# Out-projection weights and first token pairs, prepared in half-tile steps inside the last merge

## The chip, the cores and the metric

The kernel runs on one core of one Trainium2 chip. The metric is the device time of one execution in microseconds (us); lower is better. Every time below comes from the kernel before: three timed runs, and one further execution taken with the hardware profiler, whose trace is the source of all durations.

The engines have these names in the profile: PE does matmuls (PEld is its weight load), DVE is the vector engine, ACT the scalar engine, POOL the general one, SP the engine whose queue issues most transfers. L161 is line 161 of the kernel. Each engine works through its own queue in a fixed order. That order is written at compile time: the framework's scheduler walks the program in the order in which it was traced, with a cost model of its own, and places an instruction when the model says that its inputs are there. What the model takes to be ready sooner than it is on the chip makes the engine wait, with everything behind it.

## The reference, cut to what matters

One inference layer over 2,048 sample tokens and 128 prompt tokens of width 1,024. Three mixers (a gated delta rule, a spatial gating unit, a Fourier mixer) run from one input projection. Their outputs are projected back to the model width, gated and added; this sum goes through one output projection, is scaled per channel, added to the input rows and normalised:

```python
pb = jnp.einsum('btnw,nwd->btnd', br, w_branch)
gt = jax.nn.sigmoid(gates.reshape(B, T, N_BRANCH, D_MODEL))
merged = jnp.einsum('btnd,btnd->btd', gt, pb)
out = jnp.einsum('btd,de->bte', merged, w_out)
...
h = h + gate * out            # gate: one row of 1024 values per request group
y = rmsnorm(h, final_g)
```

## The kernel before, in words

All large products are done in pairs of float16 numbers: a float32 operand is scaled by a power of two and split into a high part (ACT copies it to float16) and a low part (DVE subtracts the high part); a product is then three matmuls (high·high, high·low, low·high). The power of two comes from a sum of squares: ACT squares the block with an accumulator, DVE casts the 128 sums to bfloat16, PE adds them over the partitions with a matrix of ones (the *scale product*, in `scales`, L178), and DVE makes the scale from the exponent bits.

**The merges (L1362).** Three passes, one per mixer branch (1, 2, then 0), each over 8 blocks of 128 channels (`db`) and, in each block, five token tiles (512, 512 and 128 tokens of the second half and 512, 512 of the first; the last pass takes the second half first). One tile is a gate product (24 matmuls against `xh`, `xl`), a sigmoid on ACT (L1389), a branch product (12 matmuls against `o16`), a scaling on DVE (L1398) and an addition on POOL (L1399). The merged rows go to DRAM (`mD`, printed as `mrg`). Weights of the following blocks are read into the two buffers `wst` and converted along the way.

**Work between the tiles of the last merge.** After each of its 40 tiles the last merge takes one step of a generator (`next(work, 0)`, L1401). First come the rest of `gate_rows` (the per-channel output gate from `w_ada`). Then `out_weights` (L1516) prepares W_out in 8 column blocks `i`:
- `block(i)` (L1457) loads the block (`ost`, 512 KB) and its gate row;
- `squared` (L1464) squares it on ACT, takes its scale product and its scale;
- `ungated` (L1473) splits the block and stores both halves in DRAM (`uD`, printed as `uw`; the prompt tile uses these), multiplies the block by the gate row and squares it again.

When all eight are done, one more sum and scale product (`osc`, L1528) give the scale of the gated W_out, and `quarters` (L1491) forms seven weight matrices from the four quarters of W_out: a product of a 2×2 block matrix in seven block products instead of eight. Four of them stay in SBUF (`gq`), three go to DRAM (`twD`, printed as `tw`). The float16 results of `squared`, `ungated` and `stored` all come from one tag `t16` with two buffers.

`kept` (`tc.keep_in_program_order`) pins an instruction behind what was traced before it on its engine. In the kernel before, ACT and DVE work on W_out is pinned; the scale products on PE are not.

**The out-projection (L1623).** Sixteen sample tiles are taken in eight pairs. For each pair `m_load` reads the merged rows, `m_scale` makes the pair's scale, POOL forms four sums (`pair_sums`, L1559), `pair_operands` (L1570) splits seven operands into `xl`, and seven products of 12 matmuls each (`formed`) are joined on DVE into the input rows `ha`, `hb` (L1658), which then get their norm. Pair 0 is loaded and summed near the end of the last merge, as soon as its half is stored (`ahead_out`, L1588). Pair 1, the input rows, the `tw` matrices and the final norm's row are loaded after the merge; pair 1 and the rows into a pool `op` that opens only then. The prompt tile (16) is an ordinary product with the blocks from `uD`, at the end.

Of the kernel before, what the change touches and what calls it, by code (L numbers as in the profile page):

```python
# [10 lines left out]
F32 = mybir.dt.float32  # L11
# [100 lines left out]
def hybrid_flow_kernel(ctx: ExitStack, tc: tile.TileContext, x_prompt, x_sample, state_delta, c, c_ctx, ln_g, w_ada,  # L112
# [47 lines left out]
    def mm(out, l, r, start=True, stop=True):  # L160
        PE.matmul(out, l, r, start=start, stop=stop)  # L161
# [16 lines left out]
    def scales(ss, pl, tag, sb16=None):  # L178
# [4 lines left out]
        V.tensor_copy(t[:, 0:1], ps)  # L183
# [1178 lines left out]
    def merge(n, first, inv, each=None, halves=HALVES, mid=None, then=None, work=iter(())):  # L1362

        steps, sinv = iter(()), None
        for db in range(KT):
# [8 lines left out]
            for h0, hn, tbs in halves:  # L1374
# [5 lines left out]
                for t0, tn in tbs:  # L1380
# [7 lines left out]
                    with tc.high_priority():  # L1388
                        A.activation(sg, ps, AF.Sigmoid, scale=gw.inv)  # L1389
                    ps = bank(ps_mm, [P, tn])  # L1390
# [66 lines left out]
    def block(i):  # L1457
        st = sb(orp, [P, KT, P], "ost", bufs=3)
        SY.dma_start(st, w_out[0][:, i * P:(i + 1) * P].rearrange("(k p) c -> p k c", p=P))
        gr = sb(orp, [P, P], "ogr", bufs=3)  # L1460
        SY.dma_start(gr, gateD[0:1, i * P:(i + 1) * P].to_broadcast([P, P]))
        return i, st, gr.rearrange("p (o c) -> p o c", o=1).to_broadcast([P, KT, P])

    def squared(i, st, gr):  # L1464
        ss = sb(orp, [P, 1], "uss", bufs=2)
        kept(A.activation(half16(), st, AF.Square, accum_out=ss))
        us_, inv = scales(ss, orp, "usc2")
        V.tensor_copy(uinv[:, i:i + 1], inv)
        us1 = sb(orp, [P, 1], "us1", bufs=2)
        V.tensor_copy(us1, us_)  # L1470
        return i, st, gr, us1

    def ungated(i, st, gr, us_):  # L1473
        hi, lo = half16(), half16()
        kept(A.activation(hi, st, AF.Copy, scale=us_))
        kept(V.scalar_tensor_tensor(lo, st, us_, hi, ALU.mult, ALU.subtract))
        for l, t in enumerate((hi, lo)):
            SY.dma_start(uD[i][:, l], t.rearrange("p k c -> p (k c)"))
        kept(V.tensor_tensor(st, st, gr, ALU.mult))
        kept(A.activation(half16(), st, AF.Square, accum_out=wos[:, i:i + 1]))  # L1480

    def paired(hi, lo, src):
        kept(A.copy(hi, src))
        kept(V.tensor_tensor(lo, src, hi, ALU.subtract))

    def stored(n, j, src):
        t = sb(orp, [P, 2, 4, P], "t16", F16, bufs=2)
        paired(t[:, 0], t[:, 1], src)
        SY.dma_start(twD[:, n, j], t.rearrange("p l k c -> p (l k c)"))

    def quarters(i, st, gr):  # L1491
        j = i % 4
        kept(V.scalar_tensor_tensor(st, st, wsc[0], gr, ALU.mult, ALU.mult))
        if i < 4:
            paired(gq[:, 0:2, j, 0], gq[:, 0:2, j, 1], st.rearrange("p (n k) c -> p n k c", n=2))
            yield
            return
        x_, y_ = st[:, 0:4], st[:, 4:8]
        sub = lambda out, a, b: kept(V.tensor_tensor(out, a, b, ALU.subtract))
        paired(gq[:, 2, j, 0], gq[:, 2, j, 1], y_)  # L1500
        t = sb(ep, [P, 4, P], "st", bufs=3)
        sub(t, y_, x_)
        stored(1, j, t)
        yield
        sub(x_, x_, gq[:, 0, j, 0])
        sub(x_, x_, gq[:, 0, j, 1])
        stored(0, j, x_)
        sub(y_, y_, x_)
        yield
        paired(gq[:, 3, j, 0], gq[:, 3, j, 1], y_)  # L1510
        sub(x_, gq[:, 1, j, 0], y_)
        kept(V.tensor_tensor(x_, x_, gq[:, 1, j, 1], ALU.add))
        stored(2, j, x_)
        yield

    def out_weights():  # L1516
        for _ in gates:
            yield
        read, sq = None, None
        for i in range(KT + 2):  # L1520
            was, sq = sq, squared(*read) if read is not None else None
            read = block(i) if i < KT else None
            if was is not None:
                ungated(*was)
            yield
        order_ = [0, 4, 1, 5, 2, 6, 3, 7]
        nxt = block(order_[0])
        V.tensor_reduce(wos[:, KT:KT + 1], wos[:, 0:KT], AX.X, ALU.add)  # L1528
        wsc.extend(scales(wos[:, KT:KT + 1], orp, "osc"))
        yield  # L1530
        for i in order_[1:] + [None]:
            now, nxt = nxt, block(i) if i is not None else None
            yield from quarters(*now)
# [4 lines left out]
    def m_load(t, pl, tag):  # L1538
        mt = sb(pl, [P, KT, P], tag, bufs=4 if tag == "mt" else 2)
        SY.dma_start(mt, mD[:, :, t * P:(t + 1) * P].rearrange("k p t -> p k t"))  # L1540
        return mt

    def m_scale(mts, by=None):
        jk = half16()
        ss = sb(orp, [P, 3], "mss", bufs=2)
        for i, mt in enumerate(mts):
            A.activation(jk, mt, AF.Square, accum_out=ss[:, i:i + 1])
        if len(mts) > 1:
            V.tensor_add(ss[:, 2:3], ss[:, 0:1], ss[:, 1:2])
        s, inv = scales(ss[:, 2:3] if len(mts) > 1 else ss[:, 0:1], orp, "msc")  # L1550
        minv = sb(orp, [P, 1], "minv", bufs=3)
        V.tensor_copy(minv, inv) if by is None else V.tensor_mul(minv, inv, by)
        return s, minv
# [5 lines left out]
    def pair_sums(a, b):  # L1559
        s, minv = m_scale([a, b], wsc[1])  # L1560
        yield
        sf = [sb(orp, [P, 2, 4, P], "ost", bufs=3) for _ in range(2)]
        a11, a12, a21, a22 = a[:, 0:4], a[:, 4:8], b[:, 0:4], b[:, 4:8]
# [6 lines left out]
    def pair_operands(i, a, b, sf, s, minv):  # L1570
        v = xl.rearrange("p k t -> p (k t)")[:, (i % 2) * 7168:(i % 2 + 1) * 7168].rearrange("p (l s k c) -> p l s k c", l=2, s=7, k=4)
        operands.append((v, minv))
        halved(v[:, 0, 0:2].rearrange("p s k c -> p (s k) c"), v[:, 1, 0:2].rearrange("p s k c -> p (s k) c"), a, s)
        yield
# [3 lines left out]
        halved(v[:, 0, 2], v[:, 1, 2], b[:, 4:8], s)  # L1578
# [18 lines left out]
    tw = xh.rearrange("p k t -> p (k t)")[:, 0:12288].rearrange("p (n j l k c) -> p n j l k c", n=3, j=4, l=2, k=4)  # L1597
    for n in range(3):
        SY.dma_start(tw[:, n].rearrange("p j l k c -> p j (l k c)"), twD[:, n])
    op = pool(ctx, "op", 2)  # L1600
    loaded = [m_load(t, op, "mt") for t in PAIRS[1]]

    def rows_of(t):
        hh = sb(op, [P, D], "hh", bufs=5)
        SY.dma_start(hh, xrows(t * P, P))
        return hh
# [16 lines left out]
    for i_, (ta, tb) in enumerate(PAIRS):  # L1623
# [5 lines left out]
        def coming():  # L1629
            if i_ == 0:  # L1630
                yield from pair_sums(*loaded)
            nx = [m_load(t, op, "mt") for t in PAIRS[i_ + 2]] if i_ + 2 < len(PAIRS) else None
# [49 lines left out]
        if i_ == len(PAIRS) - 3:  # L1682
            mt = m_load(16, op, "mt")
            s, minv = m_scale([mt])
            mh, ml = half16(), half16()
            halved(mh, ml, mt, s)
# [7 lines left out]
        if i_ >= len(PAIRS) - 2:  # L1694
            for i in range(4):
# [49 lines left out]
```

## Time and profile before

| | us |
|---|---|
| timed runs: median of 3 | 2208.57 |
| lowest, highest | 2205.6, 2211.82 |
| the profiled execution's own time | 2209.94 |
| its span (first to last instruction) | 2208.2 |
| PE busy in the span | 2110.2 |
| DVE, ACT, POOL busy | 1404.9, 1054.3, 728.7 |

The span ends with the last output transfer; the 1.7 us between the span and the execution's own time lie around it. The last merge runs from about 1735 to 2024 us, the out-projection from there to the end. A wait is put down to the engine and line that ended it. "PEclk" is the clock that the power control granted to PE, 1.00 being full speed.

### The profile page before, as it was taken

The page shows a single profiled execution, that of the slowest core. Times are in us where ns is not written, and L with a number is a line of the kernel's source. Part 1 is how long each engine was busy: PE and PEld are TensorE (multiplying, and loading weights), DVE is VectorE, ACT ScalarE, POOL GpSimd, SP SyncE. Part 2 cuts the span into 40 slices and gives each one's busy share as a digit, 9 for nine tenths or more (in the row PEclk, how much of TensorE's full clock was granted, in tenths as well). Part 3 has the DMA queues.
Part 4 walks back from the last instruction along what each step waited for, and adds up shares of the span by engine and source line. Part 5 has one row for each costly group of instructions (what it writes and reads, how often), then busy time and mean ns, then how long its engine had stood idle before and what let it go on. Part 6 is the DMA issues. An engine that isn't in the chain of part 4 may idle for free.

```text
span 2208.2 us, 43079 instructions
## 1 busy us (share of the span) xinstructions
PE 2110.2 (96%) x16275; PEld 1212.1 (55%) x16275; DVE 1404.9 (64%) x3229; ACT 1054.3 (48%) x2419; POOL 728.7 (33%) x870
## 2 busy tenths in 40 slices
PE   7999999999999998999899999999999999799898
PEld 3564444455555587877455565556554444344344
DVE  5736745479879698666655556756664534763874
ACT  3545644445565474554544445655543324322541
POOL 1421433223334325332322323345432212123742
PEclk9999999999999999999999999999999999999999
DMA  8424733277787664534655556766755535546552
GB/s 280 145 81 163 256 105 109 70 211 230 230 252 224 189 186 149 145 124 130 204 175 148 168 172 184 244 197 199 212 165 169 169 109 191 170 151 208 174 172 106
DMA packets 321403, 384.54 MB, mean 174 GB/s; under 512 B 40641, under 2 KB 227242, under 8 KB 318762
## 3 DMA queue, kind: packets, MB, share of 16 engines
q1 hardware_dynamic: 306058, 321.59, 47.4%
q0 software_dynamic: 12688, 51.27, 6.4%
q10 hardware_dynamic: 2448, 8.91, 1.0%
q8 instruction: 128, 2.10, 0.4%
q14 instruction: 81, 0.66, 0.1%
HBM read 246.72 MB, written 134.96 MB: 173 GB/s over the span
## 4 chain that ended last, share of the span: by engine, by line
PE 41%; DVE 8%; DMA 7%; ACT 3%; issue 2%; POOL 1%; SPq 0%; DVEq 0%; POOLq 0%; ACTq 0%
PE b L161 41%; DMA mt<-mrg 1%; DMA wst<-in_w_in_dram 1%; DMA st<-br 1%; DMA ES<-ei 1%; DVE xl L1557 1%; DMA wst<-in_w_branch_dram 1%; DMA mrg<-mrow 0%; DVE XB L797 0%; DVE E L798 0%; DVE hh L1658 0%; DVE sg L386 0%; DVE big L1360 0%; DMA ost<-in_w_out_dram 0%; DVE wlo L223 0%
## 5 line engine op out<-in xcount | busy, mean ns | idle before, releaser
L161 PE MATMUL b<-xh,whi 128*128 128x512 f16 (+1 forms) x1920 | 651.7, 348 | 2.5 <-ACT sg L1389 1.7
L161 PE MATMUL b<-xl,whi 128*128 128x512 f16 (+1 forms) x1920 | 652.2, 348 | 0.0
L161 PE MATMUL b<-xh,wlo 128*128 128x512 f16 (+1 forms) x1920 | 651.2, 348 | 0.0
L161 PEld LDWEIGHTS <-whi 128*128 128x128 f16 x3840 | 351.7, 98 | 323.0 <-issue 11.3
L161 PEld LDWEIGHTS <-wlo 128*128 128x128 f16 x1920 | 188.2, 98 | 175.1 <-issue 2.6
L161 PE MATMUL b<-big,bhi 128*128 128x512 f16 (+1 forms) x960 | 250.3, 348 | 4.9 <-ACT bhi L222 2.6
L161 PEld LDWEIGHTS <-xl 128*128 128x128 f16 x1488 | 139.4, 98 | 111.3 <-issue 21.5
L1399 POOL TENSOR_TENSOR mrow<-mrow,sg 128x512 f32<-128x512 f32 (+1 forms) x80 | 102.2, 1280 | 288.5 <-DVE sg L1398 218.9
L161 PE MATMUL b<-big,blo 128*128 128x512 f16 (+1 forms) x480 | 163.1, 347 | 0.0
L646 POOL TENSOR_TENSOR cy<-cy,raw 128x545 f32<-128x545 f32 (+1 forms) x48 | 74.4, 1576 | 183.6 <-ACT raw L645 183.6
L1389 ACT ACTIVATE sg<-b,winv 128x512 f32<-128x512 f32 (+1 forms) x120 | 74.2, 618 | 126.8 <-PE b L161 126.2
L161 PEld LDWEIGHTS <-xh 128*128 128x128 f16 x1496 | 117.7, 98 | 28.0
L161 PEld LDWEIGHTS <-bhi 128*128 128x128 f16 x960 | 86.5, 98 | 81.0 <-ACT bhi L222 3.3
L1398 DVE SCALAR_TENSOR_TENSOR sg<-b,binv,sg 128x512 f32<-128x512 f32 (+1 forms) x80 | 53.3, 667 | 77.1 <-PE b L161 76.4
L209 ACT ACTIVATE wlo<-wst 128x1024 f16<-128x1024 f32 x52 | 55.0, 1059 | 97.7 <-DMA wst<-in_w_in_dram 95.5
L866 POOL COPY T<-ES 32x256 f16<-32x256 f16 x68 | 29.5, 434 | 217.3 <-DMA ES<-ei 213.0
L175 DVE CAST wscb<-wss 128x1 bf16<-128x1 f32 x85 | 13.1, 154 | 128.8 <-ACT wlo L209 80.8
L161 PE MATMUL b<-whi,xh 128*128 128x128 f16 x544 | 94.1, 220 | 0.0
L161 PE MATMUL b<-wlo,xh 128*128 128x128 f16 x544 | 94.1, 220 | 0.0
L161 PE MATMUL b<-whi,xl 128*128 128x128 f16 x544 | 94.0, 220 | 0.0
L223 DVE SCALAR_TENSOR_TENSOR wlo<-wst,wsc,whi 128x1024 f16<-128x1024 f32 x52 | 70.6, 1363 | 28.7 <-ACT whi L222 28.6
L161 PE MATMUL b<-gq,xl 128*128 128x512 f16 x384 | 86.3, 380 | 2.5 <-DVE hh L1658 1.2
(482 smaller groups left out, 4297.4 us busy)
## 6 DMA issues: line engine op xcount, KB each, us to landing
wst<-in_w_in_dram SPq DMA_DIRECT2D x60, 512.0 KB
qkv<-cy POOLq DMA_DIRECT2D x12, 1089.0 KB, 5.2
st<-br SPq DMA_DIRECT2D x48, 256.0 KB
mrow<-mrg SPq DMA_DIRECT2D x16, 576.0 KB
mrg<-mrow POOLq DMA_DIRECT2D x16, 576.0 KB, 3.7
dc<-dec SPq DMA_DIRECT2D x17, 512.0 KB
kq<-qkv SPq DMA_DIRECT2D x34, 256.0 KB
kv<-tok POOLq DMA_DIRECT2D x17, 512.0 KB, 5.2
```

The costliest lines, as they stand in the source:

```text
L161: PE.matmul(out, l, r, start=start, stop=stop)
L175: V.tensor_copy(sb16, ss)
L209: A.activation(w.lo, st, AF.Square, accum_out=ss)
L223: V.scalar_tensor_tensor(w.lo, st, s, w.hi, ALU.mult, ALU.subtract)
L646: G.tensor_tensor(y[:, c0:c1], y[:, c0:c1], raw[:, 1 + c0:1 + c1], ALU.mult)
L866: G.tensor_copy(T16[rows(a0, b), :, :, b], ES[0:32, :, 2 * a0 + b, :, wT])
L1389: A.activation(sg, ps, AF.Sigmoid, scale=gw.inv)
L1398: V.scalar_tensor_tensor(sg, ps, binv[:, 1:2], sg, ALU.mult, ALU.mult)
L1399: G.tensor_tensor(mr, mr, sg, ALU.add)
L1557: V.scalar_tensor_tensor(lo, src, s, hi, ALU.mult, ALU.subtract)
```

## The change

Five edits, all in the last merge and the out-projection.

1. The generator gets two steps per tile instead of one: a second `next(work, 0)` stands between the sigmoid and the branch product.
2. The work on W_out is cut into smaller steps. `measured` does per block what `squared` and `ungated` did, in seven steps with empty ones between a load and its use, a new block starting every two steps; `quarters` takes blocks `j` and `j + 4` together in twelve steps, a new pair every seven. The high part (ACT) and the low part (DVE) of a split stand in different steps. The results of the squares, which nobody reads, go to tag `st` of another pool (three buffers) and no longer to `t16`.
3. The scale products of W_out and of the pairs are pinned in program order on PE (`keep=True`).
4. Pair 1 is loaded in the merge as well, right behind pair 0, as four half tiles into the buffers `whi` and `wlo` of the weights. The squares, scale and sums of pair 0 become the last steps of the generator. Squares and the split of a tile's own rows are done by halves of 512 columns.
5. The input rows of pair 0 go into the free tail of `xh` and are issued on SP first; the three `tw` loads, every later row load and the loads of the `uD` blocks are queued behind one another with `issue_after`.

```diff
-        mm(ps, ones16, widened(ss, pl, tag) if sb16 is None else sb16)
+        summed_ = mm(ps, ones16, widened(ss, pl, tag) if sb16 is None else sb16)
+        if keep:
+            tc.keep_in_program_order(summed_)
...
                     with tc.high_priority():
                         A.activation(sg, ps, AF.Sigmoid, scale=gw.inv)
+                    next(work, 0)
                     ps = bank(ps_mm, [P, tn])
...
+    def measured(i):
+        st, gr = block(i)
+        yield
+        yield
         ss = sb(orp, [P, 1], "uss", bufs=2)
-        kept(A.activation(half16(), st, AF.Square, accum_out=ss))
-        us_, inv = scales(ss, orp, "usc2")
-        V.tensor_copy(uinv[:, i:i + 1], inv)
+        kept(A.activation(sb(ep, [P, KT, P], "st", F16, bufs=3), st, AF.Square, accum_out=ss))
+        yield
+        us_, inv = scales(ss, orp, "usc2", keep=True)
         us1 = sb(orp, [P, 1], "us1", bufs=2)
         V.tensor_copy(us1, us_)
+        V.tensor_copy(uinv[:, i:i + 1], inv)
+        yield
         hi, lo = half16(), half16()
+        kept(A.activation(hi, st, AF.Copy, scale=us1))
+        SY.dma_start(uD[i][:, 0], hi.rearrange("p k c -> p (k c)"))
+        yield
+        kept(V.scalar_tensor_tensor(lo, st, us1, hi, ALU.mult, ALU.subtract))
+        SY.dma_start(uD[i][:, 1], lo.rearrange("p k c -> p (k c)"))
         kept(V.tensor_tensor(st, st, gr, ALU.mult))
+        yield
+        kept(A.activation(sb(ep, [P, KT, P], "st", F16, bufs=3), st, AF.Square, accum_out=wos[:, i:i + 1]))
...
+    def staggered(gens, by):
+        live, n = [], 0
+        while live or n < len(gens):
+            if n < len(gens) and (not live or live[-1][1] >= by):
+                live.append([gens[n], 0])
+                n += 1
+            for g_ in list(live):
+                g_[1] += 1
+                if next(g_[0], 1):
+                    live.remove(g_)
+            yield

     def out_weights():
         for _ in gates:
             yield
...
+        yield from staggered([measured(i) for i in range(KT)], 2)
+        yield
+        kept(V.tensor_reduce(wos[:, KT:KT + 1], wos[:, 0:KT], AX.X, ALU.add))
+        yield
+        wsc.extend(scales(wos[:, KT:KT + 1], orp, "osc", keep=True))
+        yield
+        yield from staggered([quarters(j) for j in range(4)], 7)
...
     def m_scale(mts, by=None):
         jk = half16()
...
         for i, mt in enumerate(mts):
-            A.activation(jk, mt, AF.Square, accum_out=ss[:, i:i + 1])
+            kept(A.activation(jk[:, 0:4], mt, AF.Square, accum_out=ss[:, i:i + 1]))
+        V.tensor_reduce(ss[:, 4:5], ss[:, 0:n], AX.X, ALU.add)
+        yield
+        s, inv = scales(ss[:, 4:5], orp, "msc", keep=True)
...
     def ahead_out(h0):
         if h0:
-            run(pair_sums(*[m_load(t, wp, "wst") for t in PAIRS[0]]))
-
-    work = out_weights()
+            first_.extend(m_load(t, wp, ["wst"]) for t in PAIRS[0])
+            loaded.extend(m_load(t, wp, ["whi", "wlo"]) for t in PAIRS[1])
+
+    def prepared():
+        yield from out_weights()
+        while not first_:
+            yield
+        yield
+        yield from pair_sums(*first_)
+
+    work = prepared()
     merge(0, False, inv_, None, HALVES[::-1], ahead_out, work=work)
     ms_.close()
+    run(work)
...
+    rows0 = [xhf[:, 12288 + 2048 * i:14336 + 2048 * i].bitcast(F32) for i in range(2)]
+    for r_, t in zip(rows0, PAIRS[0]):
+        lead = [SY.dma_start(r_, xrows(t * P, P)).ins]
     for n in range(3):
-        SY.dma_start(tw[:, n].rearrange("p j l k c -> p j (l k c)"), twD[:, n])
+        with tc.issue_after(lead[0]):
+            lead = [SY.dma_start(tw[:, n].rearrange("p j l k c -> p j (l k c)"), twD[:, n]).ins]
     op = pool(ctx, "op", 2)
-    loaded = [m_load(t, op, "mt") for t in PAIRS[1]]

     def rows_of(t):
+        if rows0:
+            return rows0.pop(0)
         hh = sb(op, [P, D], "hh", bufs=5)
-        SY.dma_start(hh, xrows(t * P, P))
+        with tc.issue_after(lead[0]):
+            lead[0] = SY.dma_start(hh, xrows(t * P, P)).ins
         return hh
...
         if i_ >= len(PAIRS) - 2:
+          with tc.issue_after(lead[0]):
             for i in range(4):
```

More of the change, by code (lines that the diff above doesn't have):

```diff
@@ L160, in mm @@
     def mm(out, l, r, start=True, stop=True):
-        PE.matmul(out, l, r, start=start, stop=stop)
+        return PE.matmul(out, l, r, start=start, stop=stop)
     def mm3(out, l, r):
@@ new lines, in measured, with quarters, gated, fresh @@
+        SY.dma_start(uD[i][:, 0], hi.rearrange("p k c -> p (k c)"))
+        yield
+        kept(V.scalar_tensor_tensor(lo, st, us1, hi, ALU.mult, ALU.subtract))
+        SY.dma_start(uD[i][:, 1], lo.rearrange("p k c -> p (k c)"))
+        kept(V.tensor_tensor(st, st, gr, ALU.mult))
+        yield
+        kept(A.activation(sb(ep, [P, KT, P], "st", F16, bufs=3), st, AF.Square, accum_out=wos[:, i:i + 1]))
+    def quarters(j):
+        sub = lambda out, a, b: kept(V.tensor_tensor(out, a, b, ALU.subtract))
+        def gated(st, gr):
+            kept(V.scalar_tensor_tensor(st, st, wsc[0], gr, ALU.mult, ALU.mult))
+        def fresh():
+            return sb(orp, [P, 2, 4, P], "t16", F16, bufs=2)
+        def keep(n, t, src):
+            low(t[:, 1], src, t[:, 0])
+            SY.dma_start(twD[:, n, j], t.rearrange("p l k c -> p (l k c)"))
+        left, right = block(j), block(j + 4)
+        yield
+        yield
+        gated(*left)
+        yield
+        st = left[0].rearrange("p (n k) c -> p n k c", n=2)
+        paired(gq[:, 0:2, j, 0], st)
+        gated(*right)
+        yield
+        low(gq[:, 0:2, j, 1], st, gq[:, 0:2, j, 0])
+        x_, y_ = right[0][:, 0:4], right[0][:, 4:8]
+        paired(gq[:, 2, j, 0], y_)
@@ L1501, in quarters @@
         t = sb(ep, [P, 4, P], "st", bufs=3)
         sub(t, y_, x_)
-        stored(1, j, t)
         yield
+        low(gq[:, 2, j, 1], y_, gq[:, 2, j, 0])
+        t3 = fresh()
+        paired(t3[:, 0], t)
         sub(x_, x_, gq[:, 0, j, 0])
         sub(x_, x_, gq[:, 0, j, 1])
-        stored(0, j, x_)
+        yield
+        keep(1, t3, t)
+        t1 = fresh()
+        paired(t1[:, 0], x_)
         sub(y_, y_, x_)
         yield
-        paired(gq[:, 3, j, 0], gq[:, 3, j, 1], y_)
+        keep(0, t1, x_)
@@ L1511, in quarters @@
+        paired(gq[:, 3, j, 0], y_)
+        yield
+        low(gq[:, 3, j, 1], y_, gq[:, 3, j, 0])
         sub(x_, gq[:, 1, j, 0], y_)
         kept(V.tensor_tensor(x_, x_, gq[:, 1, j, 1], ALU.add))
-        stored(2, j, x_)
         yield
+        t4 = fresh()
+        paired(t4[:, 0], x_)
+        yield
+        keep(2, t4, x_)
+    def staggered(gens, by):
[8 more added lines that the diff above has]
+                    live.remove(g_)
+            yield
@@ L1518, in out_weights @@
             yield
[L1519 to L1529, printed above, removed]
-        yield
-        for i in order_[1:] + [None]:
-            now, nxt = nxt, block(i) if i is not None else None
-            yield from quarters(*now)
+        yield from staggered([measured(i) for i in range(KT)], 2)
+        yield
+        kept(V.tensor_reduce(wos[:, KT:KT + 1], wos[:, 0:KT], AX.X, ALU.add))
+        yield
+        wsc.extend(scales(wos[:, KT:KT + 1], orp, "osc", keep=True))
+        yield
+        yield from staggered([quarters(j) for j in range(4)], 7)
         for i in range(2):
@@ L1559, in pair_sums @@
     def pair_sums(a, b):
-        s, minv = m_scale([a, b], wsc[1])
+        yield from m_scale([*a, *b], wsc[1])
+        s, minv = scaled
         yield
         sf = [sb(orp, [P, 2, 4, P], "ost", bufs=3) for _ in range(2)]
-        a11, a12, a21, a22 = a[:, 0:4], a[:, 4:8], b[:, 0:4], b[:, 4:8]
+        (a11, a12), (a21, a22) = a, b
         G.tensor_tensor(sf[0][:, 0], a21, a22, ALU.add)
@@ L1572, in pair_operands @@
         operands.append((v, minv))
-        halved(v[:, 0, 0:2].rearrange("p s k c -> p (s k) c"), v[:, 1, 0:2].rearrange("p s k c -> p (s k) c"), a, s)
-        yield
+        for kk in range(2):
+            halved(v[:, 0, kk], v[:, 1, kk], a[kk], s)
+            if kk:
+                yield
         for h in range(2):
@@ L1577, in pair_operands @@
             yield
-        halved(v[:, 0, 2], v[:, 1, 2], b[:, 4:8], s)
+        halved(v[:, 0, 2], v[:, 1, 2], b[1], s)
         yield
@@ L1682, in hybrid_flow_kernel @@
         if i_ == len(PAIRS) - 3:
-            mt = m_load(16, op, "mt")
-            s, minv = m_scale([mt])
+            mt = m_load(16, op, ["mt"])
+            run(m_scale(mt))
+            s, minv = scaled
             mh, ml = half16(), half16()
-            halved(mh, ml, mt, s)
+            for kk in range(2):
+                halved(mh[:, 4 * kk:4 * kk + 4], ml[:, 4 * kk:4 * kk + 4], mt[kk], s)
             inv8 = sb(orp, [P, KT], "inv8")
```

64 lines of the change are left out of this document (27 added, 37 removed).

## The prediction

> **What bounds the kernel now.** I read the page first, then busy time by stretches, then who PE waited for, then the chain and the single queues around each hole.
>
> ```profile
> span 2208.2 us, 43079 instructions
> ## 1 busy us (share of the span) xinstructions
> PE 2110.2 (96%) x16275; PEld 1212.1 (55%) x16275; DVE 1404.9 (64%) x3229; ACT 1054.3 (48%) x2419; POOL 728.7 (33%) x870
> ```
> ```profile
> 1735.00:2024.00 289.00, 272.00 (x1476) 130.16 (x1474) 142.14 (x334) 95.06 (x155) 66.88 (x61) 0.98 0.48 154
> 2024.00:2200.00 176.00, 161.66 (x872) 77.41 (x872) 124.28 (x189) 71.59 (x105) 87.75 (x73) 0.97 0.51 171
> 1750.00:1800.00 50.00, 49.56 (x282) 23.90 (x281) 22.10 (x60) 9.35 (x16) 10.40 (x11) 1.00 0.39 121
> 1890.00:1900.00 10.00, 9.47 (x38) 4.03 (x39) 4.76 (x10) 3.33 (x6) 0.00 (x0) 0.81 0.64 181
> 2030.00:2040.00 10.00, 5.86 (x27) 2.52 (x26) 2.51 (x7) 2.30 (x4) 3.29 (x3) 1.00 0.84 275
> 2040.00:2050.00 10.00, 10.00 (x40) 4.22 (x39) 8.02 (x12) 5.92 (x8) 8.49 (x7) 0.83 0.94 305
> 2070.00:2080.00 10.00, 8.25 (x37) 3.60 (x37) 9.86 (x14) 8.68 (x13) 9.29 (x6) 1.00 0.37 107
> 2080.00:2090.00 10.00, 5.42 (x17) 2.06 (x17) 7.03 (x16) 3.23 (x4) 5.64 (x6) 0.66 0.70 247
> 2090.00:2140.00 50.00, 50.00 (x236) 22.62 (x234) 36.90 (x60) 23.68 (x36) 27.23 (x24) 1.00 0.45 141
> ```
>
> The columns are the stretch, its length, busy time and instructions of PE, PEld, DVE, ACT and POOL, then PE's granted clock, the DMA share and GB/s. PE is the bound: 96% busy, and the change takes no matmul away (the pinned scale products are the same ones). All that can be won is time in which PE stands still or runs at a reduced clock. The last merge holds 289.0 - 272.0 = 17.0 us of idle PE, the out-projection 176.0 - 161.7 = 14.3. The reduced clock adds, estimated as busy time times the missing share: 9.47 x 0.19 = 1.8 at 1890, 10.00 x 0.17 = 1.7 at 2040, 5.42 x 0.34 = 1.8 at 2080. So 18.8 us lie in the merge and 17.8 in the out-projection, 36.6 in all: the ceiling of the gain. Everything ahead of the last merge is untouched.
>
> ```profile
> PE b L161 <- DVE oscb L175: 10.1, 1, 10.1
> PE b L161 <- ACT bhi L222: 2.6, 2, 1.4
> PE b L161 <- DVE wscb L175: 1.6, 1, 1.6
> PE b L161 <- ACT sg L1389: 1.6, 2, 0.8
> PE b L161 <- DVE osc L183: 0.2, 1, 0.2
> ```
> ```profile
> PE b L161 <- DVE mscb L175: 2.2, 1, 2.2
> PE b L161 <- DVE hh L1658: 1.0, 1, 1.0
> PE b L161 <- DVE sg L1658: 0.9, 1, 0.9
> ```
> ```profile
> PE b L161 <- DVE hh L1658: 8.9, 5, 5.0
> PE b L161 <- DVE sg L1658: 1.0, 2, 0.8
> ```
>
> Each row is who waited for whom: total, times, longest; the three fences are 1840 to 2024, 2024 to 2050 and 2050 to 2200. So there are three holes: one scale product (`oscb`) in the merge, the start of the out-projection, and late DVE results in its second and third pair.
>
> **Part 1: the W_out scale product.** The chain through the hole:
>
> ```profile
> 1881.27 1.05 ACT t L1475
> 1882.33 4.81 DMA uw<-t
> 1887.25 1.16 ACT t L1480 x2
> 1888.43 0.17 DVE wos L1528
> 1888.62 0.17 DVE oscb L175
> ```
>
> The last block's split is stored; the last square (L1480) needs one of the two `t16` buffers and so waits 4.81 us for that store; the sum, the cast and the scale product follow, and PE's queue had that product ahead of merge matmuls that were ready. In the changed program the squares write to tag `st`, so no store stands ahead of them, and `t16` is asked for twice per block, not four times. Counting the steps, the last square falls between the two products of tile 15, and the scale product behind the branch product of tile 16.
>
> ```profile
> 1761.60 0.75 DVE L1398 SCALAR_TENSOR_TENSOR sg<-b,binv,sg 128x512 f32<-128x512 f32 x1 [1.65 <-PE b L161]
> 1769.37 0.75 DVE L1398 SCALAR_TENSOR_TENSOR sg<-b,binv,sg 128x512 f32<-128x512 f32 x1 [7.02 <-PE b L161]
> ```
>
> These are two successive 512-token tiles: 7.8 us each (estimated by matmul share: 5.2 for the gate product, 2.6 for the branch product). Square and scale product are then 2.6 + 7.8 = 10.4 us of matmuls apart, against 1.16 + 0.17 + 0.17 us of work. I take the whole wait away: 10.1 + 0.2, the weight wait just behind it (2.6 - 1.4 = 1.2), and the reduced clock at 1890 (1.8): **-13.3**. What is late next are the other waits of the merge, 1.4 + 1.6 + 1.6 and small change; they stay.
>
> Of the Trainium skill, "TensorE: Matmul & The Clock Gate", section "Part 1: The HAM clock gate", says that the clock halves only after an idle window of about 3.4 us. The 10.1 us hole agrees; at 2040 the clock was 0.83 though no wait ahead of it exceeds 2.2 us (2.2 + 1.0 close together), so here the trace decides and I count that loss; by the page alone it wouldn't have come from these waits, and the sum would keep 1.7 us more.
>
> **Part 2: the pinned scale products and finer steps.** Eight products (`usc2`) now stand behind the branch product that follows their square's step. In that step ACT runs up to three pinned instructions in this order: an older block's second square, a split, the new square.
>
> ```profile
> L1475 ACT ACTIVATE t<-ost,us 128x1024 f16<-128x1024 f32 x8 | 9.1, 1137 | 4.4 <-DVE uinv L1468 3.5 <-DMA uw<-t 0.9
> L1480 ACT ACTIVATE t<-ost 128x1024 f16<-128x1024 f32 x8 | 8.4, 1055 | 15.2 <-DVE ost L1479 7.9 <-DMA uw<-t 4.9 <-issue 2.4
> L1466 ACT ACTIVATE t<-ost 128x1024 f16<-128x1024 f32 x8 | 8.4, 1046 | 0.2
> ```
> ```profile
> L386 DVE SCALAR_TENSOR_TENSOR sg<-wst,scT,sg 128x256 f32<-128x256 f32 x28 | 11.8, 479 | 4.5 <-DMA wst<-in_w_ada_dram 4.5
> ```
>
> That is 1.06 + 1.14 + 1.05 + a cast of about 0.2 = 3.4 us, behind a sigmoid, against a branch product of 2.6 us: up to 8 x 1.4 = 11 us if PE stood at each. A pin only forbids an earlier place; the scheduler's model has these ACT durations and can put the product among the next gate matmuls, and in the trace of before no `usc2` product made PE wait. So I take 0, with ends -4.6 (all the merge's other waits vanish) and +11. The gate rows run at double pace: their DVE work already stood 4.5 us behind loads of `w_ada`; with half the time between load and use that could double. PE saw almost none of it (50.00 - 49.56 = 0.44 us idle from 1750 to 1800); I take **+0.5**, from 0 to +4.5.
>
> The extra instructions (squares and splits by halves) lie on ACT and DVE, busy 95 and 142 of 289 us here, 72 and 124 of 176 later; at PE's full pace from 2090 to 2140 DVE had 13 us to spare. I cost them at nothing; without that cover it is about 1 us a pair, 8 in all.
>
> **Part 3: start of the out-projection.**
>
> ```profile
> 2017.10 2.91 SPq L1599 DMA_DIRECT2D xh<-tw  x3
> ```
> ```profile
> 2030.66 1.00 SPq L1540 DMA_DIRECT2D mt<-mrg  x2
> 2031.70 1.79 SPq L1605 DMA_DIRECT2D hh<-in_x_sample_dram  x2
> ```
> ```profile
> 2033.06 5.54 DMA hh<-in_x_sample_dram
> ```
>
> Pair 1's tiles and pair 0's rows are issued at 2030.7 and 2031.7, after the last store of the merge; the rows take 5.54 us. The `mscb` product of pair 1 sits in PE's queue and waits 2.2 us, then a row wait of 1.0. With pair 1 read in the last half of the merge and the rows in `xh`, both inputs come some 10 us earlier: **-3.2** and the clock at 2040, **-1.7**. What SP is moved past: the rows wait for the tail of `xh`, which the last gate product frees last, so the three `tw` loads behind them go out about 4 us later than 2017.1, with the rows' 1 MB ahead of them. The fourth product needs the first `tw`; three products of 12 matmuls (7.8 us) cover most of that. I take **+1**, from 0 to +4. No later row load is critical: five buffers hold two pairs.
>
> **Part 4: late DVE results.**
>
> ```profile
> L1557 DVE SCALAR_TENSOR_TENSOR xl<-ost,msc,xl 128x1024 f16<-128x1024 f32 x2 | 3.9, 1958 | 0.0
> L1557 DVE SCALAR_TENSOR_TENSOR xl<-mt,msc,xl 128x1024 f16<-128x1024 f32 (+1 forms) x2 | 2.6, 1296 | 0.0
> ```
>
> These are pair 1's splits as DVE ran them between 2044.5 and 2052: 3.9 + 2.6 = 6.5 us, among the joins. DVE has 2.51 us of work from 2030 to 2040, when they could have run, and is full at 2070 (9.86 of 10). With pair 1 early these 6.5 us fit into the stretch where DVE is idle, and the waits of 9.9 us shrink by as much: **-6.5** (from 0 to -9.9 - 1.8 of clock). The steady pace isn't DVE-bound, as the row from 2090 shows (36.9 of 50).
>
> ```profile
> L223 DVE SCALAR_TENSOR_TENSOR wlo<-wst,wsc,whi 128x1024 f16<-128x1024 f32 x52 | 70.6, 1363 | 28.7 <-ACT whi L222 28.6
> ```
>
> The two splits of `ost` took 1.96 us each, the same operation on weights 1.36, and POOL was busy beside them (8.49 of 10 at 2040). Of the Trainium skill, "SBUF — State Buffer", section "SBUF: two separate sides", says that DVE and GpSimd take one port pair in turns, as a lock, and the loser blocks. That speaks against bringing pair 1's sums on POOL close to pair 0's splits on DVE; by it four sums would cost about 4 x 0.6 = 2.4 us at the start (an estimate from the two durations above). My sum leaves this out, because DVE has more room there than that.
>
> **Sum** against the profiled execution of 2209.94 (span 2208.2 and 1.7 around it): -13.3 + 0.5 - 3.2 - 1.7 + 1 - 6.5 = -23.2, so 2186.7. The median of the runs shown is 1.4 below that execution: 2185.3, say **2185**.
>
> **Rivals.**
> *The merge's wait comes back in pieces*: the products of part 2 stand 1.4 us each, +11, about 2196. For it: ACT's three instructions don't fit a branch product. Against: no such wait before.
> *DVE stays late*: part 4 gives nothing, +6.5, and the `tw` loads come 4 us late instead of 1, together 2195. For it: DVE at 9.9 of 10 with POOL at 9.3 at 2070; against: 36.9 of 50 afterwards.
> *Slower*: the split in `measured` needs a `t16` buffer whose store has not landed (4.81 us above), and the new square and its pinned product stand behind it on ACT. If the scheduler's model has the store sooner, PE waits up to 4.8 us at each of eight products, and the clock falls after each by the 1.8 us seen at 2080: 8 x 6.6 = 53, less 23, about 2238. It turns from gain to loss when a product waits over 23.2 / 8 = 2.9 us. Against: two requests per block instead of four, 7.8 us apart.
> *It doesn't do what it says*: the scheduler moves other work into the freed places and equal waits return: 2208.
>
> **Chances.** Forecast 0.60, pieces 0.13, DVE late 0.12, no change 0.07, slower 0.08. About 0.3% (6.6 us) is what a measurement can tell here. The first three are faster: 0.85; same 0.07; slower 0.08. The range: low end the ceiling, 2208.6 - 36.6 = 2172; the high end takes in both partial cases with the bounds of part 2 and 3 on top, 2204.
>
> **What would show it.** Right: no `oscb` wait, the clock at 1.00 through the merge, the last W_out work ended some tiles before the merge does, the first two pairs without `mscb` and row waits, DVE busier from 2025 to 2040 and below 9 of 10 in pairs 1 and 2. Wrong: `usc2b` or ACT waits of over 1 us each on PE in the merge, waits for `tw` in the first pair, or the same `hh L1658` waits in the second and third pair.

## The result, and the profile after

The changed kernel takes **2188.18 us** (median of 5 runs, 2185.07 to 2190.16) against 2208.57: a ratio of 0.9907, 95% interval 0.9893 to 0.9922, or about 20 us. Its profiled execution took 2187.97 us, 21.97 less than the one before. The forecast was 2185 with a range from 2172 to 2204. The total came out as forecast; its parts did not. In experiment 1 below, one of the five runs was in a slower state of the chip (2463.10 us at a clock of 0.838), and its median is that of the other four.

Busy time by stretches, with the boundary at the last matmul of the last merge (2023.57 in the kernel before, 2002.92 in the changed one). The columns are as in the prediction; PE's idle time is the second number less the third. First the kernel before:

```profile
1735.00:2023.57 288.57, 272.00 (x1476) 130.16 (x1474) 141.82 (x333) 94.63 (x154) 66.45 (x61) 0.98 0.48 154
2023.57:2180.57 157.00, 142.27 (x650) 63.26 (x651) 116.77 (x177) 68.99 (x99) 84.59 (x69) 0.97 0.56 186
```

The changed kernel, with its page's first lines and its total:

```profile
span 2186.2 us, 43127 instructions
## 1 busy us (share of the span) xinstructions
PE 2106.8 (96%) x16275; PEld 1212.6 (55%) x16275; DVE 1411.7 (65%) x3239; ACT 1058.6 (48%) x2462; POOL 737.5 (34%) x870
```
```profile
1735.00:2002.92 267.92, 267.82 (x1471) 129.37 (x1469) 142.03 (x331) 93.46 (x157) 63.59 (x59) 1.00 0.51 160
2002.92:2159.92 157.00, 142.01 (x653) 63.28 (x653) 123.60 (x188) 73.24 (x138) 90.46 (x70) 0.98 0.57 196
```

The merge's idle time fell from 16.6 us to 0.1, and its clock is 1.00. The first 157 us of the out-projection have as much idle time as before, 15.0 against 14.7. Where it lies has changed. Who PE waited for, from 2003 to 2160 us (total, times, longest); from 1735 to 2003 the same view of the changed kernel is empty:

```profile
PE b L161 <- DVE hh L1722: 8.2, 6, 4.5
PE b L161 <- DVE xh L1722: 3.1, 1, 3.1
PE b L161 <- DVE mss L1589: 2.0, 1, 2.0
PE b L161 <- DVE sg L1722: 0.7, 1, 0.7
PE b L161 <- DVE xl L1600: 0.7, 1, 0.7
```

The `mscb` product and the rows make nobody wait any more, as forecast. The waits for joins (L1722) remain, and there is a new one of 3.1 us in the first pair. The 2.0 us put down to `mss` end with a join too: two joins run on DVE from 2064.20 to 2065.60, behind two slow splits, and PE goes on at 2065.65. DVE's queue ahead of the wait of 3.1 us, in the changed kernel (start, duration, engine, line):

```profile
2003.86 2.88 DVE L1600 SCALAR_TENSOR_TENSOR xl<-wst,msc,xl 128x512 f16<-128x512 f32 x2
2006.67 2.29 DVE L1600 SCALAR_TENSOR_TENSOR xl<-ost,msc,xl 128x1024 f16<-128x1024 f32 x1
2008.88 1.75 DVE L1600 SCALAR_TENSOR_TENSOR xl<-wst,msc,xl 128x512 f16<-128x512 f32 x1
2010.56 4.01 DVE L1600 SCALAR_TENSOR_TENSOR xl<-ost,msc,xl 128x1024 f16<-128x1024 f32 x1
2014.49 1.59 DVE L1722 SCALAR_TENSOR_TENSOR xh<-b,minv,xh 128x512 f32<-128x512 f32 x2
```

The same splits in the kernel before:

```profile
2024.35 1.28 DVE L1557 SCALAR_TENSOR_TENSOR xl<-wst,msc,xl 128x1024 f16<-128x1024 f32 x1
2025.54 3.49 DVE L1557 SCALAR_TENSOR_TENSOR xl<-ost,msc,xl 128x1024 f16<-128x1024 f32 x2
2028.95 0.74 DVE L1557 SCALAR_TENSOR_TENSOR xl<-wst,msc,xl 128x512 f16<-128x512 f32 x1
```

The splits took 2.88 + 2.29 + 1.75 + 4.01 = 10.9 us instead of 5.5, and the first join stands behind them: it starts at 2014.49, and PE stood still until 2015.28. Beside them POOL ran, almost without a gap (10.00 of 10 us busy from 2000 to 2010), pair 1's four sums, the last sum of pair 0 and the merge's last addition. Pair 1's sums come now because pair 1 is read early. PE's longest wait, 4.5 us, also ends with a join that stood behind splits. DVE's queue in the changed kernel ahead of it:

```profile
2069.61 0.14 DVE L189 TENSOR_SCALAR msc<-msc 128x1 int32<-128x1 int32 x1
2072.02 1.28 DVE L1683 SCALAR_TENSOR_TENSOR hh<-hh,hss,fg 128x1024 f32<-128x1024 f32 x1 [2.26 <-POOL hss L171]
...
2073.35 1.40 DVE L1600 SCALAR_TENSOR_TENSOR xl<-mt,msc,xl 128x512 f16<-128x512 f32 x2
2074.68 1.27 DVE L1683 SCALAR_TENSOR_TENSOR hh<-hh,hss,fg 128x1024 f32<-128x1024 f32 x1
2075.88 2.47 DVE L1600 SCALAR_TENSOR_TENSOR xl<-ost,msc,xl 128x1024 f16<-128x1024 f32 x2
2078.27 1.75 DVE L1600 SCALAR_TENSOR_TENSOR xl<-mt,msc,xl 128x512 f16<-128x512 f32 x1
2079.93 0.74 DVE L1722 SCALAR_TENSOR_TENSOR hh<-b,minv,hh 128x512 f32<-128x512 f32 x1
```

POOL's queue at that time, in the changed kernel:

```profile
2068.85 1.27 POOL L1608 TENSOR_TENSOR ost<-mt 128x512 f32<-128x512 f32 x1
2070.20 1.27 POOL L1609 TENSOR_TENSOR ost<-ost,mt 128x512 f32<-128x512 f32 x1
2071.43 0.55 POOL L171 TENSOR_TENSOR hss<-hss,mhalf 128x1 f32<-128x1 f32 x1
```

The final multiplication (L1683) stands at the head of DVE's queue and waits 2.26 us for a power (L171, 0.55 us). The power stands behind two sums of a pair that is not needed yet (1.27 us each). Behind the multiplication stand the splits and then the join for which PE waits. So two suspects of one origin: sums on POOL slow DVE's splits, and they delay the powers.

### The profile page after: what moved, and what is told of

Same layout as the page of the kernel before. It is cut to its first block, busy times and chain, and to the rows that moved or that the text cites. A ratio compares the mean times of both kernels' runs of the same rounds, so it can differ in the third digit from the quotient of the medians.

```text
span 2186.2 us, 43127 instructions
## 1 busy us (share of the span) xinstructions
PE 2106.8 (96%) x16275; PEld 1212.6 (55%) x16275; DVE 1411.7 (65%) x3239; ACT 1058.6 (48%) x2462; POOL 737.5 (34%) x870
## 4 chain that ended last, share of the span: by engine, by line
PE 43%; DVE 7%; DMA 5%; ACT 3%; issue 2%; POOL 1%; SPq 1%; DVEq 0%; POOLq 0%; ACTq 0%
PE b L161 43%; DVE xl L1600 1%; DMA st<-br 1%; DMA wst<-in_w_in_dram 1%; DMA ES<-ei 1%; DMA mrg<-mrow 1%; DVE big L1362 0%; DVE E L800 0%; DVE XB L799 0%; DMA wst<-in_w_branch_dram 0%; ACT big L1361 0%; DVE S L912 0%; DMA S<-in_state_delta_dram 0%; DVE S L1022 0%; POOL ost L1609 0%
```

## The experiments

The theory ahead of the first four runs: the merge's edits carry the whole gain. The rivals were the sum as predicted, with its part for the early pairs, and an effect of the pins. After them the question was what takes the out-projection's gain, and the theory became: POOL's sums. The idle columns come from the views of stretches, as above: PE idle from 1735 us to the last merge matmul, and in the 157 us behind it.

| kernel | median us | ratio to before, 95% | idle, merge | idle, 157 us behind |
|---|---|---|---|---|
| before | 2208.57 | 1 | 16.6 | 14.7 |
| changed | 2188.18 | 0.9907 (0.9893 to 0.9922) | 0.1 | 15.0 |
| 1 finer steps only | 2197.54 | 0.9954 (0.9939 to 0.9970) | 0.1 | 19.1 |
| 2 early pairs only | 2209.73 | 0.9996 (0.9983 to 1.0008) | 15.9 | 17.2 |
| 3 without pins | 2186.89 | 0.9900 (0.9881 to 0.9918) | 0.1 | 15.0 |
| 4 squares in t16 | 2199.15 | 0.9956 (0.9937 to 0.9975) | 7.6 | 14.6 |
| 5 tag only | 2205.67 | 0.9978 (0.9967 to 0.9988) | 13.0 | 15.7 |
| 6 late sums | 2192.53 | 0.9920 (0.9905 to 0.9935) | 0.1 | 15.9 |
| 7 no power | 2182.91 | 0.9876 (0.9861 to 0.9890) | 0.1 | 10.7 |
| 8 no sums | 2170.95 | 0.9819 (0.9798 to 0.9841) | 0.1 | 0.6 |
| 9 sums unread | 2182.85 | 0.9881 (0.9864 to 0.9899) | 0.1 | 10.1 |
| 10 sums on DVE | 2183.53 | 0.9888 (0.9869 to 0.9908) | 0.1 | 11.4 |
| 11 sums after the norm | 2185.94 | 0.9888 (0.9868 to 0.9907) | 0.1 | 10.8 |
| 12 half, after the norm | 2178.54 | 0.9863 (0.9847 to 0.9880) | 0.1 | 7.7 |

Each ratio is to runs of the kernel before on the same chip.

**1. Finer steps only**: the changed kernel without pair 1's early tiles, without rows in `xh` and without the order of issues.

```
-            loaded.extend(m_load(t, wp, ["whi", "wlo"]) for t in PAIRS[1])
+    loaded.extend(m_load(t, op, ["mt"]) for t in PAIRS[1])
```

> The changed kernel with edit 5 and the early reading of pair 1 taken back: pair 1, the input rows and the tw matrices are loaded after the merge as before; the half-tile steps, the pins and the st tag stay. Theory 'merge alone' (the whole gain is the merge's, where PE no longer stands; early pairs give nothing): 2188, within 3. Rival 'sum as predicted' (the merge gives 12.8, the early pairs 10.4): about 2196, with mscb and row waits of 3 us back at the start of the out-projection.

2197.54, near the rival's 2196. The merge is as clean as in the changed kernel, yet 4 us more are idle behind it (with waits of 10.6 for `hh`, 3.3 for `mscb` and 2.9 for `sg`). So the merge edits alone are worth about 10 us, half of the change, and the first theory falls. What they win is partly given back later: from the last merge matmul (2005.10) to the end of the span (2197.4) this kernel takes 192.3 us, against 184.6 before and 183.3 in the changed kernel.

**2. Early pairs only**: the kernel before with pair 1 read in the merge, rows in `xh`, and the order of issues; the coarse steps stay.

```
+            loaded.extend(m_halves(t) for t in PAIRS[1])
...
+    rows0 = [xhf[:, 12288 + 2048 * i:14336 + 2048 * i].bitcast(F32) for i in range(2)]
```

> The kernel before with pair 1 read early, the rows of pair 0 first and the row loads queued behind one another, W_out work left in its coarse steps and the products unpinned. Theory 'merge alone': 2206 to 2211, the oscb wait of 10 us stays, and the out-projection from the last merge matmul to the end takes 184 us as in both kernels. Rival 'sum as predicted': 2198, the out-projection 10 us shorter.

2209.73: nothing. Waits for `hh` are 13.2 us, more than before. From its last merge matmul (2023.10) to the end of the span (2208.7) it takes 185.6 us. The early pairs are worth 9 us on top of the finer steps (2197.54 to 2188.18), and here nothing shows. But this kernel also squares and splits by halves, so it doesn't separate the early reading from that extra work. Another difference is in the traces. In the first 157 us DVE's final multiplications wait for POOL's powers for 1.9 us before, 0.9 here, 11.1 in kernel 1 and 7.0 in the changed kernel. Only the last two have one more step in `m_scale`, ahead of the sums. Whether that step puts the sums ahead of the powers was not tried by itself, so what the early pairs are worth is not settled.

**3. Without pins**: `if keep:` in `scales` becomes `if keep and False:`.

> The changed kernel without the pins on the scale products (usc2, osc, msc), all else as changed. If the pins carry the merge's gain, the scheduler puts products ahead of their inputs again and PE waits return in the merge: 3 to 10 us, 2191 to 2198. If the finer steps and the st tag carry it, the trace shows no wait on a scale product over 1 us and the time is 2188, within 3.

2186.89, with the changed kernel's waits. The pins of the scale products do nothing that can be measured; part 2 had them at 0.

**4. Squares in t16**: the finer steps stay, the squares' unread results go back to `t16`.

```
-        kept(A.activation(sb(ep, [P, KT, P], "st", F16, bufs=3), st, AF.Square, ...
+        kept(A.activation(half16(), st, AF.Square, ...
```

> The changed kernel with the results of both squares back in the tag t16 (two buffers, four requests per block), so that ACT's squares wait for the stores of the splits again. If the store wait was the cause by itself: ACT waits of up to 5 us on uw stores at several blocks, PE waits in the merge, 2195 or more. If the finer steps give enough room between square and product: ACT shows the store waits, PE doesn't, 2188, within 3.

2199.15, 11 us worse. The wait for `oscb` does not come back, and ACT waits for no store; but with this buffer chain the weights of the merge's own blocks are late. Twice the second square (L1493) waits at the head of ACT's queue, 3.09 us until 1806.44 and 2.66 until 1845.19, just after the gated product on DVE ends (1806.35 and 1845.10), and the copy to `bhi` stands behind it. PE's waits in the merge of this kernel:

```profile
PE b L161 <- ACT bhi L224: 5.2, 2, 3.4
PE b L161 <- DVE usc2b L175: 1.8, 1, 1.8
PE b L161 <- DVE wsc L185: 0.5, 1, 0.5
```

**5. Tag only**: the reverse, that one edit in the kernel before.

> The kernel before with one edit: the two squares of each W_out block write their thrown-away result into a half-precision tile of the tag st instead of t16. Theory 'tag and steps together': the run with the changed kernel's steps and t16 squares lost 11.4 us of TensorE time in the merge, the changed kernel 2.9, the kernel before 19.2; if the two remove different waits, the tag alone takes the 10.1 us oscb wait and what hung on it, leaves the waits of the coarse steps (1.4 + 1.6 + 1.6 before the merge's last tiles), and the time is 2197 to 2200 us. Rival 'the tag alone is enough': the merge's loss falls below 4 us and the time is below 2194. Rival 'the tag needs the steps': with coarse steps the squares then wait for the st buffers, the oscb wait stays above 5 us and the time is above 2204.

2205.67, a gain of 0.2%. The theory's 2197 to 2200 was missed. The numbers are those of the rival "the tag needs the steps", though not by its mechanism: no square waits for an `st` buffer. PE's wait for `oscb` shrank from 10.1 to 6.5 us; the rest of its chain is the coarse step itself. First DVE's queue, then ACT's, in this kernel:

```profile
1885.49 1.28 DVE L1476 SCALAR_TENSOR_TENSOR t<-ost,us,t 128x1024 f16<-128x1024 f32 x1 [1.04 <-DMA uw<-t]
1886.81 1.23 DVE L1479 TENSOR_TENSOR ost<-ost,ogr 128x1024 f32<-128x1024 f32 x1
1889.25 0.16 DVE L1528 TENSOR_REDUCE wos<-wos 128x1 f32<-128x8 f32 x1 [1.22 <-ACT st L1480]
```
```profile
1888.07 1.06 ACT L1480 ACTIVATE st<-ost 128x1024 f16<-128x1024 f32 x1 [2.06 <-DVE ost L1479]
```

The store now holds up the low part of the last split (L1476) for 1.04 us, the gated product and the last square follow, and the product that needs them stands in PE's queue already. Of the merge's idle time (16.57 us) the tag alone takes 3.5 (to 13.03), the finer steps without it (kernel 4) 9.0 (to 7.56), both together all but 0.1.

**6. Late sums**: pair 1's four sums queued on POOL behind pair 0's first added row.

```
+        with tc.issue_after(added_[0]) if added_ else ExitStack():
             G.tensor_tensor(sf[0][:, 0], a21, a22, ALU.add)
```

> The changed kernel with GpSimd's four sums of pair 1 queued behind pair 0's first added row (line 1726), so that they no longer run beside pair 0's splits on VectorE. Theory 'the two engines slow each other': the four splits of pair 0 take about 5.5 us instead of 10.9, the 3.1 us wait for xh in pair 0 is below 0.5 us, no other wait grows, and the time is 2184 to 2185 us. Rival 'the sums are then late': the splits are short, but pair 1's later sums bring a new wait of 2 us or more in pair 1, and the time is 2187 to 2190. Rival 'the splits are long for another reason': they still take over 9 us and the time stays.

2192.53: the splits are short again and the 3.1 us wait is gone, but a wait of 3.7 us stands in pair 1, and the time is above the expected 2187 to 2190. In this kernel the splits, then the place of the new wait:

```profile
2005.61 2.97 DVE L1600 SCALAR_TENSOR_TENSOR xl<-wst,msc,xl 128x512 f16<-128x512 f32 x2
2008.50 2.47 DVE L1600 SCALAR_TENSOR_TENSOR xl<-ost,msc,xl 128x1024 f16<-128x1024 f32 x2
2010.89 0.74 DVE L1600 SCALAR_TENSOR_TENSOR xl<-wst,msc,xl 128x512 f16<-128x512 f32 x1
```
```profile
2033.35 2.28 DVE L1684 SCALAR_TENSOR_TENSOR xh<-xh,hss,fg 128x1024 f32<-128x1024 f32 x1 [1.66 <-POOL hss L171]
2035.55 0.74 DVE L1723 SCALAR_TENSOR_TENSOR hh<-b,minv,hh 128x512 f32<-128x512 f32 x1
```

2.97 + 2.47 + 0.74 = 6.2 us, where the sums beside them had made it 10.9. POOL's work only moved. Two of pair 2's sums now run straight ahead of the power, and a final multiplication of pair 0 waits 1.66 us for it, with the join for which PE waits behind it. In the changed kernel that wait was 0.42 us; the multiplication took 2.28 us there as well.

**7. No power**: the power -1/2 of the final norm is left out, so no final multiplication waits for POOL.

```
-        rsqrt(ss2, ss2, 1.0 / D, 1)
+        V.tensor_scalar(ss2, ss2, 1.0 / D, EPS, ALU.mult, ALU.add)
```

> The changed kernel with the power -1/2 on GpSimd left out of the final norm, so that the final multiplication waits for a VectorE result alone; the instructions on VectorE stay as many. In the changed kernel VectorE stood idle 7.0 us in front of final multiplications, waiting for that power, with the sums of the next pair ahead of it in GpSimd's queue. Theory 'head of VectorE's queue': those waits are what makes joins late in pairs 1 to 3, TensorE's waits for hh fall by 3 to 6 us, and the time is 2181 to 2185 us. Rival 'VectorE is full anyway, or the joins wait for TensorE': the waits move to other instructions, and the time is 2187 to 2189.

2182.91, idle time 15.0 to 10.7: as the theory of the head of DVE's queue had it. The waits for powers are worth 4.3 us of idle time. The 3.1 us wait in the first pair stayed, and so did one of 4.2.

**8. No sums**: POOL's sums are left out; the splits read the tiles' halves.

```
-        sf = [sb(orp, [P, 2, 4, P], "ost", bufs=3) for _ in range(2)]
...
+        sf = [a, b]
```

> The changed kernel with GpSimd's four sums of each pair left out: the splits read the halves of the two tiles instead, as four instructions of 512 where there were two of 1024 (16 x 0.2 us more on VectorE over the stage). It gives a bound for all that the sums cost: on GpSimd, in its queue ahead of the powers, and as slower splits on VectorE. Theory 'sums cost the out-projection its gain': by the mean times, splits and finals that ran beside GpSimd took about 14 us more than undisturbed ones over the stage, and VectorE waited 7.0 us for powers; without the sums TensorE's loss after the merge falls from about 20 us to 10 or less and the time is 2176 to 2181 us. Rival 'the joins are late by their order on VectorE': the loss falls by under 4 us, and the time is 2184 or more.

2170.95, below the range of the theory. The stretch behind the merge and DVE's groups from 2003 to 2160 us in this kernel (count, then busy us and mean ns, then idle time before them):

```profile
2002.49:2159.49 157.00, 156.40 (x872) 76.53 (x872) 119.46 (x214) 79.45 (x160) 48.03 (x44) 1.00 0.60 203
```
```profile
L1600 DVE SCALAR_TENSOR_TENSOR xl<-mt,msc,xl 128x512 f16<-128x512 f32 x42 | 30.0, 767 | 0.5 <-ACT xl L1599 0.5
L1679 DVE SCALAR_TENSOR_TENSOR hh<-hh,hss,fg 128x1024 f32<-128x1024 f32 x14 | 17.9, 1278 | 2.5 <-POOL hss L171 2.4
```

The same groups in the changed kernel:

```profile
L1722 DVE SCALAR_TENSOR_TENSOR hh<-b,minv,hh 128x512 f32<-128x512 f32 x38 | 27.7, 742 | 13.3 <-PE b L161 13.0 <-POOL hh L1726 0.2
L1600 DVE SCALAR_TENSOR_TENSOR xl<-ost,msc,xl 128x1024 f16<-128x1024 f32 x16 | 26.0, 1644 | 0.2 <-ACT xl L1599 0.2
L1600 DVE SCALAR_TENSOR_TENSOR xl<-mt,msc,xl 128x512 f16<-128x512 f32 x18 | 19.2, 1081 | 0.0
L1683 DVE SCALAR_TENSOR_TENSOR hh<-hh,hss,fg 128x1024 f32<-128x1024 f32 x12 | 17.4, 1447 | 6.4 <-POOL hss L171 6.2
```

Without the sums PE is idle for 0.6 us instead of 15.0. DVE ran 26 instructions more and was still busy for 4 us less; the split of 512 columns takes 767 ns instead of 1081.

**9. Sums unread**: kernel 8 with the sums put back, but read by nothing, and without the power.

> The kernel without the sums (2171 us), with GpSimd's four sums of each pair put back, but read by nothing: the splits go on reading the halves of the two tiles, and the power -1/2 is left out as well, so that no VectorE instruction waits for a sum or stands behind one by way of a power. Only the added rows of line 1726 still queue behind the sums. Theory 'slow beside each other': splits and finals take as long as in the changed kernel (means of 512 columns near 1.1 us, not 0.77), TensorE loses 6 to 12 us after the merge, and the time is 2176 to 2183 us. Rival 'it was the waits for sums and powers': although the splits are slow, the joins are in time, the loss stays under 4 us and the time is 2170 to 2174.

2182.85, idle time 10.1: the sums cost 9.5 us though no DVE instruction waits for one, and for the added rows queued behind them the joins into `hh` waited for 0.3. The splits of `mt` took 896 ns on average and those of `wst` 1532 (kernel 8: 767 and 886), so they slowed less evenly than the 1.1 us expected. The rival is out. Slow splits and final multiplications (9.5) and waits for powers (4.3) together make 13.8 of the 14.4 us between the changed kernel and kernel 8.

**10. Sums on DVE**: `G.` becomes `V.` in the four sums.

> The changed kernel with the four sums of each pair on VectorE instead of GpSimd; it computes the whole. It adds 32 sums of 0.68 to 0.75 us to VectorE, 3 us a pair, and takes away what the sums cost beside it: about 2 us a pair of slow splits and finals and 1 us a pair of waits for powers. Theory 'the sums' place was the cost': VectorE comes to about 140 of the 157 us of the stage but is never slowed, the loss after the merge falls from about 20 us to 5 to 10, and the time is 2174 to 2182 us. Rival 'VectorE is now the bound': joins stand behind the added sums, the loss stays at 16 us or more, and the time is 2186 or more.

2183.53, between the two expectations; the interval overlaps the changed kernel's, so a gain isn't shown. DVE is busy for 37.4 of the 40 us from 2040, and joins stand behind the added sums. Two of the four sums took 1.02 and 1.04 us there on average, where 0.68 to 0.75 was expected, and the splits of `mt` 855 ns: POOL's added rows still run beside them.

**11. Sums after the norm**: one step later, and queued on POOL behind the last power.

```
+        yield
+        with tc.issue_after(powers[-1]) if powers else ExitStack():
```

> The changed kernel with the sums of a pair queued on GpSimd behind the last power of the pair in work, one step later than before; it computes the whole. If the waits for powers (7.0 us on VectorE, worth 5 to 7 us by the run without the power) come from the sums ahead of them in GpSimd's queue, those waits fall below 3 us; the sums still run beside splits, so the theory 'slow beside each other' lets only the powers' part come back: 2182 to 2186 us. Rival 'the sums are then late': splits of sums wait on VectorE with joins behind them, and the time is 2188 or more.

2185.94, as expected; by its interval not told apart from the changed kernel. The wait for powers at full-width final multiplications fell from 6.2 to 2.5 us, but these took 1699 ns instead of 1447: the sums found them there.

**12. Half, after the norm**: kernel 11 with the last two of the four sums on DVE.

> The changed kernel with both remedies by halves: GpSimd keeps the first two sums of each pair, queued behind the last power of the pair in work, and VectorE takes the other two; it computes the whole. If slow splits beside GpSimd cost about 12 us and waits for powers 5 to 7 of the 20 us lost after the merge, half of the first and most of the second come back, and VectorE pays 12 us of its own time, of which it had over 25 to spare: 2178 to 2183 us, under both sums on VectorE alone (2183.5) and sums behind the norm alone (2185.9). Rival 'VectorE's order decides': its sums wait for GpSimd's at the head of VectorE's queue with joins behind them, and the time is 2184 to 2190.

2178.54, as expected. Its interval (0.9847 to 0.9880) lies below the changed kernel's (0.9893 to 0.9922), so it is faster than that kernel as well as than the one before. Its interval overlaps those of kernels 10 and 11. The stretch behind its merge:

```profile
1998.55:2155.55 157.00, 149.27 (x694) 67.01 (x695) 135.11 (x213) 75.61 (x140) 70.48 (x57) 0.99 0.58 196
```

POOL is busy for 70.5 us instead of 90.5, DVE for 135.1 instead of 123.6, and 7.7 us are idle instead of 15.0.

## Why the prediction was right in total and wrong in its parts

**Part 1 was right and too small.** The `oscb` wait, the weight wait behind it and the reduced clock went. The step that failed is "the other waits of the merge, 1.4 + 1.6 + 1.6 and small change; they stay". They went too: 16.5 us of idle time and 1.8 of clock, 18.3, where parts 1 and 2 had -12.8. Experiments 4 and 5 show why: with squares in `t16`, ACT and DVE work on W_out delays the merge's own weights; with coarse steps, `oscb` as well. Only both edits together clear it. The end of part 2 at which "all the merge's other waits vanish" was the true one. That the last W_out work ended early is seen too: its last copy on ACT starts at 1950.4, 53 us ahead of the merge's end (before: 1992.3, 31 us).

**Neither the rival of part 2 nor the slow one came.** No `usc2b` product made PE wait in the changed kernel; in experiment 4 one did, for 1.8 us.

**Part 3's waits went, and another took their place.** The 2.2 us for `mscb` and 1.0 for rows are gone and no `tw` matrix came late. But pair 1 read early brings its sums early, beside pair 0's splits, and those cost 3.1 us.

**Part 4 failed: -6.5 forecast, nothing measured.** The step was "these 6.5 us fit into the stretch where DVE is idle, and the waits of 9.9 us shrink by as much". The waits put down to joins are 8.2 + 3.1 + 0.7 us, no less than before. The stretch wasn't free: pair 0's slow splits filled it until 2014.5, and pair 1's splits stand behind them. Their first and last in the changed kernel:

```profile
2020.71 0.75 DVE L1600 SCALAR_TENSOR_TENSOR xl<-whi,msc,xl 128x512 f16<-128x512 f32 x1 [0.54 <-ACT xl L1599]
2027.01 1.76 DVE L1600 SCALAR_TENSOR_TENSOR xl<-wlo,msc,xl 128x512 f16<-128x512 f32 x1
```

They start 17.8 us behind the last merge matmul, against 21.3 before (2044.90), and the five of them take 6.7 us. From the last merge matmul to the end of the span it is 184.6 us before and 183.3 after: 1.3 us less, where parts 3 and 4 had 10.4. The mechanism of the rival "DVE stays late" held; the merge's surplus of 5.5 us, and 2.3 us ahead of 1735 us, where the change touches nothing, hid it in the total: 18.3 + 1.3 + 2.3 = 21.9 of 21.97. That the total fits is luck.

**The extra instructions, put at nothing, are an open end.** With the finer steps alone the out-projection grew by 7.7 us (experiment 1), about the 8 that part 2 named for them without cover. No run separates them from the new order of POOL's queue.

**What my sum left out was the price.** I estimated pair 1's sums beside pair 0's splits at 2.4 us and left them out of the sum "because DVE has more room there than that". The splits took 5.4 us more, of which experiment 6 won back 4.7 by moving those sums, and experiment 9 puts the slowing over the stage at 9.5 us of PE time. Room by busy share is no room for an instruction whose result is due: DVE was at 8 of 10 from 2070 to 2080, "below 9" as I had written, while PE waited 4.5 us for it.

The Trainium skill, "SBUF — State Buffer", section "SBUF: two separate sides", names the condition that I had not weighed: two inputs in SBUF on DVE, against a GpSimd instruction that reads SBUF. The traces agree: splits and final multiplications took longer in the changed kernel than in kernel 8 (1081 against 767 ns, 1447 against 1278), while joins, which read a PSUM bank, took 742 ns in the changed kernel and 743 to 744 in kernels 8 and 9.

## What to carry to other kernels

An engine's idle stretch is not free if the work moved into it meets another engine's work that slows it; ask what else comes early with the same data. A queue's head matters more than its busy share: for each late result, list what stands ahead of it, and for each of these what it waits for on the other engine. A total that comes out right proves little until its terms are compared one by one.

## What the hardware showed

Beside POOL, DVE's splits often grow by the same amount whatever their width: 0.74 to 1.75 us at 512 columns, 1.28 to 2.29 at 1024, about 1.01 in both. Others at 1024 lie between (1.84 and 1.93 us in the changed kernel) or above (4.01). The clock after a wait did not follow the wait's length alone. In the changed kernel a hole of 3.1 us left it at 1.00, and one of 4.5 us was followed by 0.50:

```profile
2015.00:2020.00 5.00, 4.72 (x23) 2.16 (x23) 3.69 (x11) 0.05 (x1) 1.27 (x1) 1.00 0.85 216
...
2080.00:2085.00 5.00, 4.28 (x11) 1.48 (x11) 2.11 (x6) 0.00 (x0) 2.59 (x3) 0.50 0.80 260
```

In kernel 9 a wait of 2.3 us from 2010 was followed by 0.85, and one of 3.7 us that ended at 2076.33 left the clock at 1.00:

```profile
2010.00:2015.00 5.00, 2.67 (x9) 0.96 (x8) 4.51 (x7) 0.00 (x0) 1.77 (x3) 0.80 0.34 133
2015.00:2020.00 5.00, 5.00 (x22) 2.09 (x21) 2.00 (x7) 0.72 (x2) 1.00 (x1) 0.85 1.00 260
...
2075.00:2080.00 5.00, 3.67 (x17) 1.66 (x17) 4.89 (x10) 0.00 (x0) 2.24 (x1) 1.00 0.89 276
```

The rule of about 3.4 us that the prediction cited from the Trainium skill ("TensorE: Matmul & The Clock Gate", section "Part 1: The HAM clock gate") agrees with the first two and not with these two. What else decides was not tried.
